# Weight splits, the order of the last pair, and out-projection weights through DRAM in the first layer of a streaming Conformer kernel

## Chip, cores and metric

The kernel runs on one core of a Trainium2 chip. The metric is the device time of one execution in microseconds (us). TensorE (PE), VectorE (DVE), ScalarE (ACT), GpSimd (POOL) and the queue of SyncE (SP), which issues nearly all DMAs, each work through their own list of instructions in order and wait for one another by semaphores.

## Reference

A two-layer encoder on 4096 prompt rows and 64 sample rows of width 1024. Only its first layer is touched by the change:

```
h = rmsnorm(x, pre_g)
z = h @ w_in + b_in                      # 1024 -> 3 x 1024
a, gl, gate = jnp.split(z, 3, axis=-1)
u = a * jax.nn.sigmoid(gl)
u_hist = jnp.concatenate([hist, u], axis=1)
c = depthwise_conv(u_hist, w_dw) + b_dw  # causal, 31 taps per channel
c = silu(layernorm(c, ln_g, ln_b)) * silu(gate)
y = c @ w_out + b_out
x = x + rmsnorm(y, post_g)
```

The second layer is sliding-window attention on the result, with its own projections.

## The kernel before

Every fp32 matrix is held as two fp16 parts, a high half and a low half, and each product is three fp16 matmuls (`mm3`): high by high, high by low, low by high. A weight's high half is a scaled copy by ACT or POOL (L161, L159), and its low half is one operation of DVE (L162) that reads the staged fp32 weight and the high half.

**Projections.** The prompt is cut into 8 blocks of 512 rows, taken two at a time: pair 0 is blocks 0 and 1, and so on to pair 3. For each block `in_jobs` loads four tiles of 128 rows (`x`), takes their norm, scales them (ACT, L483) and transposes them on PE (L207) into `hT`. A slot is one projection of 128 output channels for one block: 24 matmuls with 512 columns. Per channel group j (8 of them) there are three: `gl` (the gate of the gated unit; ACT takes the sigmoid, `sig`), `a` (the value; DVE multiplies it with `sig` into `u`, L774) and `gt` (the output gate; ACT takes the silu, `sg`, and a DMA puts it into `g_scr`). Three PSUM buffers carry the projections (`ps_mm`). `order(p)` writes the order of slots by hand: 48 in a pair. In pair 3 the eight `gt` slots of the second block are taken out into `tail`, after everything else.

**Convolution.** When both blocks of a pair have their `u` for group j, `conv_jobs` queues 31 taps over 1024 columns. Eleven go through ACT (products, L605) and POOL (adds into `pacc`, L614). Then ACT seeds the PSUM accumulator `acc` (L623, one buffer), and DVE adds 19 taps (L630), adds `pacc` (`join`, L641) and a DMA stores the result in `c_scr`. There are four buffers for `u`. `pump` doles out queued taps slot by slot, so the convolution of a pair runs on into the next pair.

**Other work at given slots.** `wjobs` gives the slot in pair 0 at which a quarter of a weight is loaded and split (`load_wa`: two loads of 512 KB into staging tiles `wst`, then eight high and eight low halves). `sched` gives the slots at which the rows of the next pair are loaded, normed, scaled and transposed. `big` (6 buffers) and `quad` (8 buffers) are pools of 4 KB per partition that staging tiles, `x`, `hT` and others share.

**Tail and layer norm.** After pair 3's slots, each of the eight `tail` slots is followed by one `w_oa_job` (load and split a piece of the out-projection weight, in the space where `w_a` was). `la_iter` runs the layer norm and out-projection of each 128 rows as a pipeline of steps (sums on POOL, statistics on PE into `lnb`, L264 to L317 on DVE, silu and the high half `hl` on ACT, L302 and L312, then products `psy`). Its first iterations stand in the last pair (`LA_LAST`) and the tail (`LA_TAIL`).

Within these rules a scheduler places the instructions of each engine at compile time, so neighbours on one engine may come from different slots.

## Time and profile before

| | us |
|---|---|
| median of three runs (2910.94, 2910.99, 2918.94) | 2910.99 |
| profiled execution | 2917.75 |
| its span, from first to last instruction | 2915.3 |
| PE busy in the span | 2765.5 |
| DVE busy in the span | 2251.6 |
| POOL busy in the span | 1680.8 |

In the span, pair 0 begins with the first projections at about 13.5 us, pair 3 ends and the tail begins at about 1075, the first `psy` product begins at 1124.1, and the second layer fills the stretch from about 1500 to the end. Rows of a profile give a start, a duration, the engine, the line, and the tiles written and read; "x8" is a count of instructions, and an arrow in brackets names what the engine waited for.

### The profile page before, as it was taken

The page shows a single profiled execution, that of the slowest core. Times are in us where ns is not written, and L with a number is a line of the kernel's source. Part 1 is how long each engine was busy: PE and PEld are TensorE (multiplying, and loading weights), DVE is VectorE, ACT ScalarE, POOL GpSimd, SP SyncE. Part 2 cuts the span into 40 slices and gives each one's busy share as a digit, 9 for nine tenths or more (in the row PEclk, how much of TensorE's full clock was granted, in tenths as well). Part 3 has the DMA queues.
Part 4 walks back from the last instruction along what each step waited for, and adds up shares of the span by engine and source line. Part 5 has one row for each costly group of instructions (what it writes and reads, how often), then busy time and mean ns, then how long its engine had stood idle before and what let it go on. Part 6 is the DMA issues. An engine that isn't in the chain of part 4 may idle for free.

```text
span 2915.3 us, 62257 instructions
## 1 busy us (share of the span) xinstructions
PE 2765.5 (95%) x24441; PEld 1793.6 (62%) x24441; DVE 2251.6 (77%) x3828; ACT 1785.7 (61%) x3957; POOL 1680.8 (58%) x1614
## 2 busy tenths in 40 slices
PE   7988999999999998999988999999999999999998
PEld 5433455444444443444447998998777777777775
DVE  5899888989988889979975777754676666666665
ACT  5666667666666566457764777654555555555554
POOL 4888578779877798977742344323334333333332
PEclk9999999999999999999999999999999999999999
DMA  5122111121120124666645666667323323433321
GB/s 169 53 80 69 53 54 49 39 68 48 46 80 29 44 67 139 207 189 188 207 155 174 211 207 222 209 198 233 99 94 113 115 99 99 128 104 96 114 72 60
DMA packets 256010, 341.16 MB, mean 117 GB/s; under 512 B 40069, under 2 KB 184197, under 8 KB 254949
## 3 DMA queue, kind: packets, MB, share of 16 engines
q1 hardware_dynamic: 255717, 337.20, 36.0%
q8 instruction: 191, 3.13, 0.4%
q14 instruction: 102, 0.84, 0.1%
HBM read 206.46 MB, written 130.72 MB: 116 GB/s over the span
## 4 chain that ended last, share of the span: by engine, by line
PE 32%; DVE 8%; ACT 5%; DMA 4%; POOL 2%; issue 2%; SPq 1%; POOLq 0%; ACTq 0%; DVEq 0%
PE sx_g L991 5%; PE psy L182 3%; PE psy L183 3%; PE psy L185 3%; PE sz_g L991 3%; PE ptr L1610 2%; PE pv L1644 2%; PE sx_q L991 2%; ACT p L1575 2%; PE sz_q L991 2%; PE sw_g L991 1%; PE sc L1544 1%; PE sc L1545 1%; DVE tTb L1112 1%; DVE x L1097 1%
## 5 line engine op out<-in xcount | busy, mean ns | idle before, releaser
L630 DVE SCALAR_TENSOR_TENSOR acc<-u,pt,acc 128x1024 f32<-128x1024 f32 x608 | 782.1, 1286 | 60.9 <-ACT acc L623 47.0
L614 POOL TENSOR_TENSOR pacc<-pacc,prods 128x1024 f32<-128x1024 f32 x213 | 505.9, 2376 | 105.6 <-ACT prods L605 95.3
L605 ACT ACTIVATE prods<-u,pt 128x1024 f32<-128x1024 f32 x213 | 241.9, 1144 | 94.6 <-POOL pacc L614 94.0
L1575 ACT ACTIVATE p<-p,st 128x192 f32<-128x192 f32 (+1 forms) x520 | 228.1, 441 | 80.6 <-DVE st L1569 80.2
L614 POOL TENSOR_TENSOR pacc<-pacc,pr 128x1024 f32<-128x1024 f32 x107 | 253.9, 2373 | 39.0 <-ACT pr L605 34.0
L182 PE MATMUL psy<-w_oa,hl 128*128 128x512 f16 x512 | 198.7, 388 | 20.4 <-ACT hl L312 14.9
L1548 DVE CUSTOM_DVE_ANT_0 p<-sc,bias 128x192 f32<-128x192 f32 (+1 forms) x520 | 159.7, 349 | 73.8 <-PE sc L1545 56.6
L1594 POOL TENSOR_TENSOR p<-p,st 128x768 f32<-128x768 f32 (+2 forms) x130 | 190.1, 1483 | 34.4 <-DVE st L1590 33.2
L190 PE MATMUL ps_gt<-hT,w_gt 128*128 128x512 f16 x512 | 197.0, 385 | 10.1 <-ACT w_gt L161 5.3
L192 PE MATMUL ps_a<-hT,w_a 128*128 128x512 f16 (+1 forms) x528 | 198.1, 375 | 3.2 <-DVE w_a L162 3.2
L183 PE MATMUL psy<-w_oa,hl 128*128 128x512 f16 x512 | 198.4, 388 | 2.1 <-DVE w_oa L162 2.1
L190 PE MATMUL ps_a<-hT,w_a 128*128 128x512 f16 (+1 forms) x528 | 198.1, 375 | 2.1 <-ACT sig L793 1.7
L190 PE MATMUL ps_gl<-hT,w_gl 128*128 128x512 f16 (+1 forms) x528 | 198.5, 376 | 1.7 <-ACT sig L793 1.1
L191 PE MATMUL ps_gl<-hT,w_gl 128*128 128x512 f16 (+1 forms) x528 | 197.9, 375 | 0.9 <-DVE hT L209 0.9
L192 PE MATMUL ps_gt<-hT,w_gt 128*128 128x512 f16 x512 | 195.8, 383 | 2.8 <-DVE w_gt L162 2.8
L191 PE MATMUL ps_a<-hT,w_a 128*128 128x512 f16 (+1 forms) x528 | 198.1, 375 | 0.0
L192 PE MATMUL ps_gl<-hT,w_gl 128*128 128x512 f16 (+1 forms) x528 | 197.9, 375 | 0.0
L182 PE MATMUL psy<-w_ob,ogT 128*128 128x512 f16 x512 | 195.1, 381 | 2.4 <-ACT ogT L1660 2.4
L191 PE MATMUL ps_gt<-hT,w_gt 128*128 128x512 f16 x512 | 196.9, 385 | 0.0
L183 PE MATMUL psy<-w_ob,ogT 128*128 128x512 f16 x512 | 195.1, 381 | 0.0
L991 PEld LDWEIGHTS <-w_qS 128*128 128x128 f16 x3072 | 180.2, 100 | 12.0 <-issue 11.7
L991 PEld LDWEIGHTS <-w_gS 128*128 128x128 f16 x3072 | 180.7, 98 | 6.0 <-issue 4.8
(363 smaller groups left out, 7120.6 us busy)
## 6 DMA issues: line engine op xcount, KB each, us to landing
x<-in_x_prompt SPq DMA_DIRECT2D x32, 512.0 KB, 3.4
g_scr<-sg SPq DMA_DIRECT2D x64, 256.0 KB, 2.0
c_scr<-c SPq DMA_DIRECT2D x32, 512.0 KB, 2.6
c<-c_scr SPq DMA_DIRECT2D x32, 512.0 KB, 4.5
g<-g_scr SPq DMA_DIRECT2D x32, 512.0 KB, 4.2
x<-x_scr SPq DMA_DIRECT2D x128, 128.0 KB, 3.6
h_scr<-hTb SPq DMA_DIRECT2D x32, 512.0 KB, 3.5
h_scr<-tTb SPq DMA_DIRECT2D x32, 512.0 KB, 4.7
```

Source lines behind the costliest of these rows:

```text
L182: nc.tensor.matmul(out, wts[i][0], mov[i][0], start=i == 0, stop=False)
L183: nc.tensor.matmul(out, wts[i][0], mov[i][1], start=False, stop=False)
L190: nc.tensor.matmul(out, wh, mh, start=i == 0, stop=False)
L191: nc.tensor.matmul(out, wh, ml, start=False, stop=False)
L192: nc.tensor.matmul(out, wl, mh, start=False, stop=i == n - 1)
L605: nc.scalar.activation(dst[:, :T], u[:, k : k + T], AF.Identity, scale=wdw[:, j, k : k + 1], bias=pt[:, j, R_DWB : R_DWB + 1] if k == 0 el ...
L614: nc.gpsimd.tensor_tensor(out=pacc[:, :T], in0=pacc[:, :T], in1=dst[:, :T], op=ALU.add)
L630: nc.vector.scalar_tensor_tensor(out=acc[:, :T], in0=u[:, k : k + T], scalar=wdw[:, j, k : k + 1], in1=acc[:, :T], op0=ALU.mult, op1=ALU.add,)
L991: nc.tensor.matmul(ps[:, j, :], w[:, wz, kb, j * P : j * P + P], rhs(rz, kb), start=first and j + kb + wz + rz == 0, stop=last and j == KH ...
L1548: nc.vector.tensor_tensor_reduce(out=pbuf[:, t, par * 192 + lo : par * 192 + 192], in0=ps[:, tt, :nk], in1=bias[:, lo:], scale=1.0, scalar ...
L1575: nc.scalar.activation(pp, pp, AF.Exp, scale=2.0 ** -(kv * 4 + t) / SQ, bias=st[:, 1, par, t : t + 1], accum_out=st[:, 3, par, t : t + 1],)
L1594: nc.gpsimd.tensor_tensor(out=pp, in0=pp, in1=st[:, 4, par, :, None].to_broadcast([P, 4, 3 * CH - lo]), op=ALU.mult)
```

## The change

1. The weights of `w_in` are split sooner: the ten quarters of `w_in` are loaded at slots 0, 2, 3, 5, 9, 12, 14, 16, 24 and 27 in place of 1, 7, 7, 8, 13, 19, 19, 20, 31 and 32. Those before slot 17 are staged in `quad` tiles, not `big` ones.
2. The convolution of groups 0 and 1 in pair 0 is done in two halves of 512 columns (`HALVES`), the first of them as soon as the first block's `u` is there.
3. In every pair but the last, groups 6 and 7 of the first block come before those of the second. In the last pair all `gl` and `a` come first, then the eight `gt` of the first block, then those of the second as before.
4. Loads, norms, scales and transposes of the next pair's rows get other slots; for the second block the scale is taken apart from the transposes by two slots.
5. The out-projection weight is split in pairs 1 and 2 instead of in the tail: `put_w_oa` loads a piece of 256 KB into a `big` tile, splits it into another (16 pieces, eight in each pair) and stores both halves in a DRAM scratch. In pair 3, at slot 32, four DMAs of 1 MB fetch them. The state output of the sample (`state_out`) moves from the end of pair 1 to slot 3 of pair 2.

```
+HALVES = 2
-LA_LAST = {36: -6, 39: -5, 43: -4}
+LA_LAST = {33: -6, 36: -5, 39: -4}
-OA_TAIL = (1, 1, 1, 1, 1, 1, 1, 1)
...
-        for g in range(4):
-            wjobs.setdefault(6 * g + 1, []).append(lambda g=g: load_wa(w_gt, 2 * D, 256 * g, 256))
-            if g < 3:
-                wjobs.setdefault(12 * g + 7, []).append(lambda g=g: load_wa(w_gl, D, 256 * (g + 1), 256))
-                wjobs.setdefault(12 * g + 8, []).append(lambda g=g: load_wa(w_a, 0, 256 * (g + 1), 256))
+        for m, dst, base, g in (
+            (0, w_gt, 2, 0), (2, w_gl, 1, 1), (3, w_a, 0, 1), (5, w_gt, 2, 1), (9, w_gt, 2, 2),
+            (12, w_gl, 1, 2), (14, w_a, 0, 2), (16, w_gt, 2, 3), (24, w_gl, 1, 3), (27, w_a, 0, 3),
+        ):
+            args = (dst, base * D, 256 * g, 256, quad if m < 17 else None)
+            wjobs.setdefault(m, []).append(lambda args=args: load_wa(*args))
 
         def order(p):
             out = []
+            if p == SB // 2 - 1:
+                out = [(k, h, j) for j in range(KB) for h in range(2) for k in ("gl", "a")]
+                return out + [("gt", h, j) for h in range(2) for j in range(KB)]
...
+            out += [(k, 0, j) for j in range(KB - 2, KB) for k in ("gl", "a")] + [("gt", 1, j) for j in range(4, 6)]
+            out += [(k, 1, j) for j in range(KB - 2, KB) for k in ("gl", "a")] + [("gt", 1, j) for j in range(6, 8)]
             return out
...
-                conv_jobs(b // 2, j, u, TC)
+                if b == 1 and j < HALVES:
+                    conv_jobs(0, j, u, TA, TA, True)
+                else:
+                    conv_jobs(b // 2, j, u, 0, TC, True)
+            elif b == 0 and j < HALVES:
+                conv_jobs(0, j, u, 0, TA, False)
...
+        def put_w_oa(g, k):
+            box = {}
+
+            def load():
+                t = box["t"] = big([P, D], F32, f"woa_{g}_{k}")
+                nc.sync.dma_start(out=t[:, :HN], in_=woa_v[:, k, g * HN : g * HN + HN])
+                box["w"] = big([P, 2, HN], F16, f"woas_{g}_{k}")
+
+            def comp():
+                st, w = box["t"][:, :HN], box["w"]
+                nc.scalar.activation(w[:, 0], st, AF.Copy, scale=SW)
+                nc.vector.scalar_tensor_tensor(
+                    out=w[:, 1], in0=st, scalar=SW, in1=w[:, 0], op0=ALU.mult, op1=ALU.subtract
+                )
+                nc.sync.dma_start(out=woa_scr[k // KH * 2 + g, :, :, k % KH, :], in_=w)
...
-                    for z, fn in zip((10, 13, 15, 16, 16), (a_[1][i], a_[2][i]) + a_[3][i]):
-                        sched.setdefault(z + 6 * i, []).append(fn)
...
+                    for z, fn in zip((14, 16, 19, 20, 20), (a_[1][i], a_[2][i]) + a_[3][i]):
+                        sched.setdefault(z + 5 * i, []).append(fn)
...
+            if p in (1, 2):
+                for z in range(8):
+                    load, comp = put_w_oa(p - 1, z)
+                    sched.setdefault(2 + 3 * z // 2, []).append(load)
+                    sched.setdefault(3 + 3 * z // 2, []).append(comp)
...
+                if p + 1 == NP and m == 2 * 2 * KB:
+                    w_oa = Weight("w_oa")
+                    for k in range(2):
+                        for g in range(2):
+                            nc.sync.dma_start(out=w_oa.t[k][g], in_=woa_scr[2 * k + g])
```

The lists of instructions show what this moves. The first place is DVE near its first convolution tap in pair 0. Names are tile, block or pair, group and a running number, so `u_0_0` is the first `u`, `acc_0_0` its accumulator, `w_gt_01` a piece of the `gt` weight; L162 before is L163 after, L630 is L631, L774 is L781. Before, from the last low halves ahead of the taps:

```order
L162 SCALAR_TENSOR_TENSOR w_a_10_81<-wst_817,gsc_73,w_a_10_81 128x256 x4
L774 SCALAR_TENSOR_TENSOR u_0_0_531<-ps_a_1_0_736,ba_109,sig_1_0_694 128x512
L162 SCALAR_TENSOR_TENSOR w_gt_01_88<-wst_1017,gsc_73,w_gt_01_88 128x256 x2
L630 SCALAR_TENSOR_TENSOR acc_0_0_798<-u_0_0_531,pt_102,acc_0_0_798 128x1024
L162 SCALAR_TENSOR_TENSOR w_gt_01_88<-wst_1017,gsc_73,w_gt_01_88 128x256 x2
L630 SCALAR_TENSOR_TENSOR acc_0_0_798<-u_0_0_531,pt_102,acc_0_0_798 128x1024 x2
```

The same place after:

```order
L781 SCALAR_TENSOR_TENSOR u_0_0_532<-ps_a_0_0_483,ba_110,sig_0_0_481 128x512
L163 SCALAR_TENSOR_TENSOR w_a_10_82<-wst_638,gsc_73,w_a_10_82 128x256 x2
L163 SCALAR_TENSOR_TENSOR w_a_00_80<-wst_628,gsc_73,w_a_00_80 128x256
L210 TENSOR_TENSOR hT_1_3_334<-pst_a1_0_1_342,hT_1_1_332 128x4x128
L163 SCALAR_TENSOR_TENSOR w_gt_00_88<-wst_747,gsc_73,w_gt_00_88 128x256
L163 SCALAR_TENSOR_TENSOR w_a_10_82<-wst_638,gsc_73,w_a_10_82 128x256
L163 SCALAR_TENSOR_TENSOR w_gt_00_88<-wst_747,gsc_73,w_gt_00_88 128x256
L163 SCALAR_TENSOR_TENSOR w_a_10_82<-wst_638,gsc_73,w_a_10_82 128x256
L163 SCALAR_TENSOR_TENSOR w_gt_00_88<-wst_747,gsc_73,w_gt_00_88 128x256
L631 SCALAR_TENSOR_TENSOR acc_0_0_553<-u_0_0_532,pt_103,acc_0_0_553 128x512
```

The first tap now follows the first block's `u` (`ps_a_0_0`), not the second's (`ps_a_1_0`); 19 low halves of 256 columns stand ahead of that first `u`, where there were none, and in all 64 of the 80 stand ahead of the first block of 1024-column taps.

The second place is DVE where the convolution of group 5 of pair 3 ends and that of group 6 runs beside the first layer-norm steps (L264, L298 and L310 before; one more after). Before:

```order
L641 TENSOR_TENSOR c_3_5_8721<-acc_3_5_8512,pacc_3_5_8464 128x1024
L630 SCALAR_TENSOR_TENSOR acc_3_6_8724<-u_6_6_8541,pt_102,acc_3_6_8724 128x1024 x2
L162 SCALAR_TENSOR_TENSOR w_oa_10_8814<-wst_8927,w_oa_10_8814 128x512 x2
L630 SCALAR_TENSOR_TENSOR acc_3_6_8724<-u_6_6_8541,pt_102,acc_3_6_8724 128x1024 x2
L282 TENSOR_SCALAR lnr_1_8971<-lnb_8624 128x1
L264 TENSOR_TENSOR c_2_8699<-c_2_8699,lnb_8624 128x1024
L298 TENSOR_TENSOR c_0_8501<-c_0_8501,lnb_8624 128x1024
```

After:

```order
L642 TENSOR_TENSOR c_3_5_8799<-acc_3_5_8637,pacc_3_5_8474 128x1024
L631 SCALAR_TENSOR_TENSOR acc_3_6_8837<-u_6_6_8471,pt_103,acc_3_6_8837 128x1024 x2
L283 TENSOR_SCALAR lnr_1_9179<-lnb_8913 128x1
L265 TENSOR_TENSOR c_2_9027<-c_2_9027,lnb_8913 128x1024
L631 SCALAR_TENSOR_TENSOR acc_3_6_8837<-u_6_6_8471,pt_103,acc_3_6_8837 128x1024
L299 TENSOR_TENSOR c_0_8788<-c_0_8788,lnb_8913 128x1024
```

The sixteen low halves of `w_oa` are gone from here, and the steps of the layer norm stand where they stood, relative to the convolution.

The third place is SP in pair 2, where pieces of the out-projection weight are loaded (L816, new) and stored (L825, new). Before, nothing of the kind stands on SP; after:

```order
L825 DMA woa_scr_79<-woas_1_0_5454 256x1x512
L816 DMA woa_1_1_5512<-in_a_w_out 128x512
L825 DMA woa_scr_79<-woas_1_1_5514 256x1x512
L816 DMA woa_1_2_5586<-in_a_w_out 128x512
L825 DMA woa_scr_79<-woas_1_2_5588 256x1x512
L816 DMA woa_1_3_5641<-in_a_w_out 128x512
L825 DMA woa_scr_79<-woas_1_3_5643 256x1x512
L816 DMA woa_1_4_5729<-in_a_w_out 128x512
L706 DMA g_scr_76<-sg_4_2_5726 128x512
L643 DMA c_scr_75<-c_1_7_5553 128x1024
```

Each load stands behind the store of the piece before it: with `hT_4` in four of the six `big` buffers, two are left for a piece and its halves. The stores of a gate (`sg_4_2`) and of a convolution result (`c_1_7`) stand behind four such loads.

More of the change, by code (lines that the diff above doesn't have):

```diff
@@ L119, in tile_streaming_conformer @@
     x1_scr = dpool.tile([NT, D], F32, name="x1_scr")
+    woa_scr = dpool.tile([4, P, 2, KH, HN], F16, name="woa_scr")
     def slot(shape, dt, name):
@@ L543, in tile_streaming_conformer, with load_wa @@
         a_w = ins["a_w_in"][0]
-        def load_wa(dst, base, c0, cn):
+        def load_wa(dst, base, c0, cn, room=None):
             step = 1024 // cn
             for k0 in range(0, KB, step):
-                st = big([P, step, cn], F32, "wst")
+                st = (room or big)([P, step, cn], F32, "wst")
                 split_weight(dst, a_w, st, list(range(k0, k0 + step)), base + c0, cn, c0, 0, True)
@@ L584, in tile_streaming_conformer, with conv_jobs @@
         LAG = 2
-        def conv_jobs(b, j, u, T):
-            t0 = bl[2 * b][0]
+        def conv_jobs(b, j, u, o, T, last):
+            t0 = bl[2 * b][0] + o
             cd = (T + 124) / 960.0
@@ L606, in run @@
                         dst[:, :T],
-                        u[:, k : k + T],
+                        u[:, o + k : o + k + T],
                         AF.Identity,
@@ L623, in seed @@
                 nc.scalar.activation(
-                    box["acc"][:, :T], u[:, k : k + T], AF.Identity, scale=wdw[:, j, k : k + 1], bias=0.0
+                    box["acc"][:, :T], u[:, o + k : o + k + T], AF.Identity, scale=wdw[:, j, k : k + 1], bias=0.0
                 )
@@ L630, in run @@
                     nc.vector.scalar_tensor_tensor(
-                        out=acc[:, :T], in0=u[:, k : k + T], scalar=wdw[:, j, k : k + 1], in1=acc[:, :T],
+                        out=acc[:, :T], in0=u[:, o + k : o + k + T], scalar=wdw[:, j, k : k + 1], in1=acc[:, :T],
                         op0=ALU.mult, op1=ALU.add,
@@ L638, in join @@
                 clock["pacc"] -= 1
-                clock["u"] -= 1
+                clock["u"] -= last
                 out = pa.tile([P, TC], F32, tag="cout", name=f"c_{b}_{j}", bufs=1)
@@ L745, in order @@
                 out += [(k, 1, j) for j in range(2) for k in ("gl", "a")] + [("gt", 0, j) for j in range(2, 4)]
-            for j in range(0 if p else 2, KB):
+            for j in range(0 if p else 2, KB - 2):
                 A, B = [("gl", 0, j), ("a", 0, j)], [("gl", 1, j), ("a", 1, j)]
@@ L795, in sig_slot @@
             )
+        woa_v = ins["a_w_out"][0].rearrange("(k p) n -> p k n", p=P)
+        def put_w_oa(g, k):
[11 more added lines that the diff above has]
+                nc.sync.dma_start(out=woa_scr[k // KH * 2 + g, :, :, k % KH, :], in_=w)
+            return load, comp
         sigs, ubox = {}, {}
@@ L803, in tile_streaming_conformer @@
             if late_prep:
-                for z, fn in zip((0, 0, 0, 1, 1, 1), late_prep):
+                for z, fn in zip((0, 0, 1, 1), late_prep):
                     sched.setdefault(z, []).append(fn)
@@ L810, in tile_streaming_conformer @@
                 for i in range(4):
-                    for z, fn in zip((10, 13, 15, 16, 16), (a_[1][i], a_[2][i]) + a_[3][i]):
-                        sched.setdefault(z + 6 * i, []).append(fn)
-                for z, i in ((39, 0), (41, 1)):
+                    for z, fn in zip((14, 16, 19, 20, 20), (a_[1][i], a_[2][i]) + a_[3][i]):
+                        sched.setdefault(z + 5 * i, []).append(fn)
+                for i, z in enumerate((34, 36, 43, 45)):
                     sched.setdefault(z, []).append(b_[1][i])
-                for i in range(2):
-                    for fn in (b_[2][i],) + b_[3][i]:
-                        sched.setdefault(44 + i, []).append(fn)
-                    sched.setdefault(45 + i, []).append(b_[1][2 + i])
-                for fn in (b_[2][2],) + b_[3][2]:
-                    sched.setdefault(47, []).append(fn)
-                late_prep = [b_[2][3], *b_[3][3]]
+                for i, z in enumerate((36, 37, 45, 46)):
+                    sched.setdefault(z, []).append(b_[2][i])
+                for i, z in enumerate((40, 41, 46, 47)):
+                    for fn in b_[3][i][:1]:
+                        sched.setdefault(z, []).append(fn)
+                for i, z in enumerate((42, 43)):
+                    for fn in b_[3][i][1:]:
+                        sched.setdefault(z, []).append(fn)
+                late_prep = [*b_[3][2][1:], *b_[3][3][1:]]
             if p == 0:
                 hTs, l, nm, tr = in_jobs(SB)
-                for z, fn in zip((36, 37, 38, 38, 38), (l[0], nm[0]) + tr[0]):
+                for z, fn in zip((30, 31, 33, 33, 33), (l[0], nm[0]) + tr[0]):
                     sched.setdefault(z, []).append(fn)
@@ L863, in tile_streaming_conformer @@
             sjobs.popleft()()
-        w_oa = Weight("w_oa")
-        oaj = deque((c0, k0) for c0 in (0, 512) for k0 in range(0, KB, 2))
-        def w_oa_job():
-            c0, k0 = oaj.popleft()
-            st = big([P, 2, 512], F32, "wst")
-            split_weight(w_oa, ins["a_w_out"][0], st, [k0, k0 + 1], c0, 512, c0, None)
         ec = [slot([P, 2, D], F32, f"early_{z}") for z in range(4)]
@@ L878, in tile_streaming_conformer @@
                 la_iter(ti, la_fns)
-            for _ in range(OA_TAIL[q_] if q_ < len(OA_TAIL) else 0):
-                if oaj:
-                    w_oa_job()
             gate_slot(*args)
@@ L885, in tile_streaming_conformer @@
             pump(dq, "d", TAIL_D)
-        while oaj:
-            w_oa_job()
         for ti in range(EARLY):
```

3 lines of the change are left out of this document (2 added, 1 removed).

## The prediction

> **What bounds the kernel now.** I read the totals first, then the busy time by stage, then what PE waited for in the stages where it loses time, then DVE in those stages.
>
> ```profile
> span 2915.3 us, 62257 instructions
> PE 2765.5 (95%) x24441; PEld 1793.6 (62%) x24441; DVE 2251.6 (77%) x3828; ACT 1785.7 (61%) x3957; POOL 1680.8 (58%) x1614
> ```
>
> PE is busy for 95% of the span, so the change can only take from PE's idle time and from its slow clock, and only in the stages that it touches. The windows show them (columns: stretch, its us, then busy us and count of PE, PEld, DVE, ACT, POOL, then PE's granted clock, DMA share, GB/s):
>
> ```profile
> 0.00:63.00 63.00, 47.66 (x272) 31.24 (x273) 35.48 (x84) 37.97 (x76) 32.52 (x60) 0.92 0.51 165
> 63.00:136.00 73.00, 73.00 (x391) 38.27 (x390) 60.25 (x58) 49.16 (x60) 60.72 (x33) 1.00 0.22 73
> 136.00:349.00 213.00, 186.66 (x936) 87.25 (x934) 200.22 (x184) 139.03 (x177) 164.10 (x97) 0.96 0.21 70
> 349.00:843.00 494.00, 491.74 (x2743) 236.91 (x2742) 439.18 (x424) 320.37 (x389) 394.42 (x235) 1.00 0.14 49
> 843.00:890.00 47.00, 40.17 (x187) 19.80 (x186) 41.46 (x37) 31.66 (x40) 36.37 (x28) 0.93 0.33 101
> 890.00:1075.00 185.00, 185.00 (x860) 84.07 (x859) 162.32 (x137) 110.87 (x119) 152.06 (x70) 1.00 0.13 43
> 1075.00:1118.00 43.00, 41.11 (x199) 19.36 (x197) 38.69 (x35) 30.40 (x42) 41.96 (x26) 1.00 0.31 98
> 1118.00:1255.00 137.00, 119.40 (x547) 56.00 (x547) 125.58 (x120) 74.45 (x135) 117.84 (x111) 0.94 0.62 194
> ```
>
> In each I take idle time (stretch less PE busy) plus the part of the stretch that the clock is short of 1.00. For 136 to 349, the body of pair 0 and the start of pair 1: 213 − 186.66 = 26.3, and 0.04 × 213 = 8.5, together **34.9**. For 843 to 890, the boundary of pairs 2 and 3: 6.8 + 3.3 = **10.1**. For 1075 to 1255, the tail and the first layer-norm products: 1.9 + 17.6 + 8.2 = **27.7**. Between them PE is full. The first 63 us lose 15 and some clock to loads and first transposes. So 72.7 us are within reach; the second layer and the rest of the first keep their instructions, and I leave them as they are. The clock is low only in the stretches with idle time, and I let it follow that time.
>
> Then what PE waited for, first from 63 to 349, then from 843 to 1255 (total us, times, longest):
>
> ```profile
> PE pst_a L207 <- ACT x L483: 8.5, 2, 4.6
> PE ps_gt L190 <- ACT w_gt L161: 5.3, 2, 3.6
> PE ps_gt L190 <- DVE u L774: 4.0, 1, 4.0
> PE ps_a L192 <- DVE w_a L162: 3.2, 4, 1.0
> PE ps_gt L192 <- DVE w_gt L162: 2.8, 2, 1.7
> PE ps_a L190 <- ACT sig L793: 1.7, 1, 1.7
> ```
>
> ```profile
> PE psy L182 <- ACT hl L312: 12.1, 6, 4.0
> PE pst_a L207 <- ACT x L483: 6.6, 2, 4.1
> PE psy L183 <- DVE w_oa L162: 2.1, 1, 2.1
> ```
>
> In pair 0 the weight halves cost 11.3, the two steps behind a late `u` or `sig` 5.7, and transposes whose rows were scaled too late 8.5. At the boundary it is transposes again. In the tail it is `hl`, the end of the layer norm's chain, which passes DVE many times; DVE is 92% busy from 1118 to 1255 (125.58 of 137) and 94% from 136 to 349. So beside the transposes **DVE is what PE waits for**, and the question is how much work leaves DVE there.
>
> **The change part by part.** *Pair 0: weights split sooner, convolution in halves.* One row for a low half alone, one for a piece beside POOL's adds, and the windows of L162 alone (busy of DVE, count, then clock, DMA share, GB/s):
>
> ```profile
> 40.00:80.00 40.00, 15.45 (x34) 1.00 0.38 119
> 80.00:260.00 180.00, 55.52 (x46) 0.97 0.21 72
> ```
>
> ```profile
> 173.53 1.27 DVE L630 SCALAR_TENSOR_TENSOR acc<-u,pt,acc 128x1024 f32<-128x1024 f32 x1
> 174.72 7.53 DVE L162 SCALAR_TENSOR_TENSOR w_a<-wst,gsc,w_a 128x256 f16<-128x256 f32 x3
> L614 POOL TENSOR_TENSOR pacc<-pacc,prods 128x1024 f32<-128x1024 f32 x213 | 505.9, 2376 | 105.6 <-ACT prods L605 95.3
> L162 DVE SCALAR_TENSOR_TENSOR w_a<-wst,gsc,w_a x16: 469/692/2575, 171.8 to 249.9; 128x256 f16<-128x256 f32 x16
> ```
>
> Ahead of the convolution a low half takes 15.45 / 34 = 0.454 us. Beside it, 55.52 / 46 = 1.207, and three of them 7.53: a low half reads two SBUF tiles, and waits out an add of 2.376. Taps, with `acc` in PSUM, stay at 1.286. All 80 cost 71.0 now. After the change 19 stand ahead of the first `u`, 45 between it and the last of the two halved groups, and 16 in the full convolution. The 45 are not free of adds: the halves bring the adds forward as well, at half the width. With m for their mean, the 80 cost 19 × 0.454 + 45m + 16 × 1.207 = 27.9 + 45m.
>
> ```profile
> 80.25 1.29 DVE L630 SCALAR_TENSOR_TENSOR acc<-u,pt,acc 128x1024 f32<-128x1024 f32 x1 [3.09 <-ACT acc L623]
> 40.00:80.00 40.00, 40.00 (x248) 24.43 (x246) 21.60 (x44) 20.98 (x35) 16.46 (x16) 1.00 0.38 119
> L630 DVE SCALAR_TENSOR_TENSOR acc<-u,pt,acc 128x1024 f32<-128x1024 f32 x608 | 782.1, 1286 | 60.9 <-ACT acc L623 47.0
> L774 DVE SCALAR_TENSOR_TENSOR u<-ps_a,ba,sig 128x512 f32<-128x512 f32 x64 | 47.7, 746 | 14.2 <-PE ps_a L192 14.2
> ```
>
> The halves cost DVE something. No tap of 512 columns is in the trace; by the row of `u`, also 512 columns with one operand in PSUM, I take 0.746. For two groups, 38 times (2 × 0.746 − 1.286) = 7.8; two seeds more at 47.0 / 28 = 1.7 (the waits for a seed at L623, all but four of the 32) = 3.4; and two joins more at some 0.2 each beyond their columns: 11.6. They also give DVE something: taps now start after the first block's `u` at 41, not at 80.25, and from 40 to 80 DVE is idle for 40 − 21.60 = 18.4. DVE's standing in pair 0 so changes by 27.9 + 45m − 71.0 + 11.6 − 18.4 = **45m − 49.9**. At m = 0.454 that is −29.5; at 2.575, with each waiting out a full add, +66. I take 0.692, the median of the row of `w_a` in pair 0, since adds at half width block for less: **−19**. At most −29 counts, since of the 34.9 the sample's transposes keep some 6 (its scale and transposes still stand in one slot: half of the 8.5, with its share of clock).
>
> *The start.* The 19 low halves ahead of the first `u` take 8.6, and the row stands next to idle time:
>
> ```profile
> 36.67 0.44 DVE L527 COPY pt<-pst_rows 128x268 f32<-128x268 f32 x1 [3.95 <-PE pst_rows L524]
> 40.33 0.75 DVE L774 SCALAR_TENSOR_TENSOR u<-ps_a,ba,sig 128x512 f32<-128x512 f32 x1 [1.91 <-PE ps_a L192]
> wst<-in_a_w_in SPq DMA_DIRECT2D x6, 512.0 KB, 8.1
> ```
>
> 5.9 of it fits in these two gaps; **+3** (bounds 0 and +8). The last row, of the DMA issues up to 40 us, has six loads, landing in 8.1; six more are issued by slot 5, behind the rows of both blocks on SP's queue.
>
> *The boundary.* Scales now stand two slots ahead of their transposes, 2 × 5.2 us by the 24 products of a slot at 0.216 (5.18). Both waits of 6.6 in total, and the clock with them, go: **−9** of 10.1. If ACT is later than two slots, nothing goes.
>
> *Out-projection pieces in pairs 1 and 2.* Sixteen low halves come to a stretch where DVE works 439.18 of 494:
>
> ```profile
> L162 DVE SCALAR_TENSOR_TENSOR w_oa<-wst,w_oa x16: 679/956/2581, 1086.8 to 1146.7; 128x512 f16<-128x512 f32 x16
> ```
>
> Each takes 0.68 alone and 2.58 beside adds, 10.9 to 41.3 in all. DVE's idle time there is 54.8, of which 16 seeds at 1.7 are not free: 27.6 are left. At 1.43 each (0.68, and the 0.75 that low halves of pair 0 gain beside adds) it is 22.9, hidden in those 27.6; I charge **+3** for pieces at bad places, bounds 0 and +14 (41.3 − 27.6). Without that cover it would be the 22.9. ACT's sixteen high halves lie in its idle time (320.37 of 494). On SP, loads wait for stores over two buffers, with gate and result stores queued behind; there are 12 slots, 62 us, for eight pieces, 7.8 each.
>
> The Trainium skill says in "SBUF — State Buffer", section "SBUF: two separate sides", that VectorE and GpSimd share one pair of ports as an exclusive lock: a VectorE operation with two SBUF inputs and a GpSimd operation that reads SBUF block each other for the whole instruction, whichever starts first. This case's trace agrees (7.53 for three). That speaks against moving this split into pairs 1 and 2, where adds are frequent: by the rule a low half among back-to-back adds waits half an add on average, 0.68 + 1.19 = 1.87, an estimate, so 29.9 for the sixteen, 7 more than the 22.9 above.
>
> *The tail.* DVE loses the sixteen low halves and their waits. In the windows they took:
>
> ```profile
> 1080.00:1150.00 70.00, 18.13 (x16) 0.93 0.47 152
> ```
>
> Also, the last `u` come eight slots earlier, 41 us, since the `gt` of the first block now follow them. DVE can use that as far as it is idle from 890 to 1075: 22.7, less six seeds at 1.7, 12. Together it enters the layer norm some 30 us ahead. But the chain of one iteration through sums, DVE and ACT to `hl` stays as long, and its first steps stand at the same places relative to the convolution; waits for `hl` of up to 4.0 may be that chain alone. I take a little over half of 27.7: **−15**, bounds −5 and −26.
>
> *Edits at nothing.* The four 1 MB fetches of `w_oa` are issued after slot 32 of pair 3, some 16 slots and the eight of the tail, 83 to 125 us, ahead of the first `psy`; the DMA share there is 0.13. At 3.8 us for 512 KB they need about 30. The moved state output and the order of groups 6 and 7 change no count; PE has its three PSUM buffers for the second.
>
> **Sum**, against the profiled execution of 2917.75: +3 − 19 − 9 + 3 − 15 = −37. That execution is 6.8 above the median 2910.99; I take the same difference from the median: **2874**, its own range 2858 to 2886.
>
> **The rivals.** *DVE stays the bound.* m is 0.82 (0.454 and a share of a half-width add), the out-projection pieces pay fully, the start too: +8 − 13 − 9 + 14 − 15 = −15, **2896**. For it: 200.22 of 213 busy. Against it: 11.3 of the waits name weights, which now come earlier whatever DVE does.
>
> *Nearly all waits go.* −29 − 10 − 26 = −65, **2846**. For it: lateness of DVE up to two slots (10.4) is taken up by three PSUM buffers, so a part of its saving counts in full. Against it: the `hl` chain.
>
> *The split is not in fact sooner.* Six more loads of 512 KB at 3.8 delay the rows behind them by up to 22.8, so the start pays 20 and pair 0 gains 14, the tail 7: 20 − 14 − 9 + 3 − 7 = −7, **2904**, within 0.3% of no change, about what a measurement can tell. For it: the DMA share of 0.51 up to 63. Against it: it is short of full, and DVE is idle beside it.
>
> *Slower.* The 45 low halves meet adds after all, since the halved groups start POOL's adds near 45 us, where the first now comes at 77.22:
>
> ```profile
> 77.22 2.36 POOL L614 TENSOR_TENSOR pacc<-pacc,prods 128x1024 f32<-128x1024 f32 x1 [0.57 <-ACT prods L605]
> ```
>
> With the out-projection pieces at their upper end too, the sum is 45m − 49.9 + 3 − 9 + 14 − 15 = 45m − 57: it turns at m = 1.27, and at 1.55 gives +13, **2924**. For it: 1.207 beside adds today, three at 2.5 in a row. The Trainium skill's rule on the shared ports, named above, is this mechanism; the trace has it for full adds only. Against it: an add of 512 columns blocks for about half as long, and the adds fill only a part of 41 to 80.
>
> **How the numbers follow.** Forecast .45, DVE stays the bound .20, nearly all gone .17, not sooner .10, slower .08. Faster by over 0.3% (below 2902) are the first three, .82; same .10; slower .08. The range goes from 2842, a little below the second rival with all terms at their best ends, to 2904, with the third at its edge; the slower case and the odd miss are left out.
>
> **What would show it.** The first tap near 50, not 80. L162 (then L163) in 40 to 100: m at 0.7 or at 1.3. No PE waits for `w_gt` or `w_a`, and for `x` only the sample's; from 136 to 349 PE idle near 12, not 26. In pairs 1 and 2 the sixteen low halves near 1.4, with no new waits of PE. In the tail no `w_oa`, waits for `hl` about half, and the first `psy` about 22 sooner than now:
>
> ```profile
> 1124.07 0.39 PE L182 MATMUL psy<-w_oa,hl 128*128 128x512 f16 x1 [1.82 <-ACT hl L312]
> ```
>
> I am wrong if PE's idle time moves to the first 63 us, if pairs 1 and 2 lose more than 5, or if the second layer moves by more than 5.

## The result and the profile after

The changed kernel takes 2891.52 us (median of four runs, 2889.01 to 2893.14), the kernel before 2914.97 in four runs; the ratio is 0.9914, 95% interval 0.9898 to 0.9930. That is 23.5 us less; the forecast was 37 less, 2874 (its own range 2858 to 2886), in a range of 2842 to 2904 for all cases together. The profiled execution took 2892.36, 25.4 below the one before.

The totals, and the busy time by stage at the same clock times as before (us, PE, PEld, DVE, ACT, POOL, PE's granted clock, DMA share, GB/s). From the middle of pair 0 on, the changed kernel is further in its work at the same clock time:

```profile
span 2890.6 us, 62399 instructions
PE 2762.4 (96%) x24441; PEld 1795.7 (62%) x24441; DVE 2248.4 (78%) x3868; ACT 1783.4 (62%) x3973; POOL 1687.3 (58%) x1634
```

```profile
0.00:63.00 63.00, 46.99 (x260) 30.68 (x261) 48.59 (x110) 45.62 (x92) 48.73 (x73) 0.89 0.73 236
136.00:349.00 213.00, 203.67 (x1034) 96.43 (x1033) 191.41 (x177) 138.59 (x179) 149.17 (x84) 0.97 0.24 80
349.00:843.00 494.00, 483.00 (x2699) 233.64 (x2698) 440.24 (x427) 323.51 (x400) 385.14 (x235) 1.00 0.17 58
843.00:890.00 47.00, 44.70 (x207) 20.70 (x206) 42.02 (x38) 32.99 (x37) 45.49 (x27) 0.96 0.24 68
1118.00:1255.00 137.00, 122.76 (x583) 59.22 (x582) 123.65 (x115) 70.87 (x135) 120.98 (x124) 0.98 0.59 178
```

In pair 0 (136 to 349) PE's idle time fell from 26.3 to 9.3. In pairs 1 and 2 (349 to 843), where PE lost 2.3, it now loses 11.0. What PE waits for, first in pair 0, then from 349 to 843, then from the tail to the end of the out-projection (total us, times, longest):

```profile
PE ps_gt L191 <- DVE u L781: 2.5, 1, 2.5
PE ps_gl L191 <- DVE u L781: 2.1, 1, 2.1
PE ps_gl L191 <- ACT hT L209: 2.1, 1, 2.1
PE ps_gt L191 <- ACT sig L805: 1.9, 1, 1.9
PE pst_a L208 <- ACT x L484: 1.7, 1, 1.7
```

```profile
PE pst_a L208 <- DVE hT L210: 3.6, 1, 3.6
PE ps_gt L191 <- ACT sig L805: 3.2, 2, 1.9
PE ps_gl L191 <- DVE u L781: 1.7, 2, 1.5
PE ps_gt L191 <- DVE u L781: 1.7, 1, 1.7
```

```profile
PE lnb L281 <- POOL csq L275: 14.6, 12, 5.5
PE psy L183 <- ACT hl L313: 7.8, 5, 2.9
```

Of the 11.0, the wait of 3.6 lies behind 800 and belongs to the boundary of pairs 2 and 3, which now comes sooner; the waits for `u` and `sig` are a loss that the kernel before did not have. No weight is waited for any more. In the tail the waits for `hl` have about halved, from 14.9 to 7.8, and those for POOL's sums of squares (`csq`) have grown from 10.9 to 14.6:

```profile
PE psy L182 <- ACT hl L312: 14.9, 7, 4.0
PE lnb L280 <- POOL csq L274: 10.9, 13, 1.3
```

Windows at equal clock times mix the stages of two kernels once one is ahead. So I also compare when the same operation ends in both traces. The u are counted from 1 to 64, 16 to a pair. Two such rows, the last u of pair 0 and the last of pair 2, in the trace before:

```profile
309.26 0.75 DVE L774 SCALAR_TENSOR_TENSOR u<-ps_a,ba,sig 128x512 f32<-128x512 f32 x1
...
852.11 0.74 DVE L774 SCALAR_TENSOR_TENSOR u<-ps_a,ba,sig 128x512 f32<-128x512 f32 x1
```

and in the trace after:

```profile
290.38 0.74 DVE L781 SCALAR_TENSOR_TENSOR u<-ps_a,ba,sig 128x512 f32<-128x512 f32 x1
...
841.73 0.75 DVE L781 SCALAR_TENSOR_TENSOR u<-ps_a,ba,sig 128x512 f32<-128x512 f32 x1
```

The lead is 18.9 at the first and 10.4 at the second. All along the program (ends in us):

| operation | before | after | difference |
|---|---|---|---|
| 3rd u | 74.7 | 81.8 | +7.1 |
| 6th u (group 2 of pair 0) | 120.5 | 122.9 | +2.4 |
| 16th u, end of pair 0 | 310.0 | 291.1 | -18.9 |
| 20th u, in pair 1 | 394.0 | 381.2 | -12.8 |
| 34th u, in pair 2 | 640.1 | 624.2 | -15.9 |
| 36th u, in pair 2 | 668.4 | 660.0 | -8.4 |
| 48th u, end of pair 2 | 852.9 | 842.5 | -10.4 |
| first output gate of the tail | 1085.3 | 1070.6 | -14.7 |
| last output gate of the tail | 1133.6 | 1112.9 | -20.7 |
| last psy | 1532.6 | 1505.7 | -26.9 |
| span | 2915.3 | 2890.6 | -24.7 |

From the 6th u on pair 0 gains 21, the tail and the out-projection 12, the stretch from the end of pair 2 to the tail 4. Pairs 1 and 2 give back 8.5, in two steps: 6 by the 20th u, and 7.5 between the 34th and the 36th; between the steps 3 are gained.

### The profile page after: what moved, and what is told of

Its sections match the earlier page's. It is cut to its first block, busy times and chain, and to the rows that moved or that the text cites. A ratio compares the mean times of both kernels' runs of the same rounds, so it can differ in the third digit from the quotient of the medians.

```text
span 2890.6 us, 62399 instructions
## 1 busy us (share of the span) xinstructions
PE 2762.4 (96%) x24441; PEld 1795.7 (62%) x24441; DVE 2248.4 (78%) x3868; ACT 1783.4 (62%) x3973; POOL 1687.3 (58%) x1634
## 5 line engine op out<-in xcount | busy, mean ns | idle before, releaser
L631 DVE SCALAR_TENSOR_TENSOR acc<-u,pt,acc 128x1024 f32<-128x1024 f32 (+1 forms) x646 | 790.7, 1224 | 73.0 <-ACT acc L624 57.2
L615 POOL TENSOR_TENSOR pacc<-pacc,prods 128x1024 f32<-128x1024 f32 (+1 forms) x227 | 510.9, 2253 | 105.8 <-ACT prods L606 89.3
L606 ACT ACTIVATE prods<-u,pt 128x1024 f32<-128x1024 f32 (+1 forms) x227 | 246.1, 1093 | 102.7 <-POOL pacc L615 102.1
L615 POOL TENSOR_TENSOR pacc<-pacc,pr 128x1024 f32<-128x1024 f32 (+1 forms) x113 | 254.5, 2253 | 42.4 <-ACT pr L606 30.7
L1580 DVE CUSTOM_DVE_ANT_0 p<-sc,bias 128x192 f32<-128x192 f32 (+1 forms) x520 | 159.7, 350 | 92.9 <-PE sc L1577 74.7
L1023 PEld LDWEIGHTS <-w_qS 128*128 128x128 f16 x3072 | 179.7, 99 | 11.9 <-issue 11.5
```

The lines of the kernel that those rows point to most:

```text
L606: nc.scalar.activation(dst[:, :T], u[:, o + k : o + k + T], AF.Identity, scale=wdw[:, j, k : k + 1], bias=pt[:, j, R_DWB : R_DWB + 1] if k ...
L615: nc.gpsimd.tensor_tensor(out=pacc[:, :T], in0=pacc[:, :T], in1=dst[:, :T], op=ALU.add)
L631: nc.vector.scalar_tensor_tensor(out=acc[:, :T], in0=u[:, o + k : o + k + T], scalar=wdw[:, j, k : k + 1], in1=acc[:, :T], op0=ALU.mult, o ...
L1023: nc.tensor.matmul(ps[:, j, :], w[:, wz, kb, j * P : j * P + P], rhs(rz, kb), start=first and j + kb + wz + rz == 0, stop=last and j == KH ...
L1580: nc.vector.tensor_tensor_reduce(out=pbuf[:, t, par * 192 + lo : par * 192 + 192], in0=ps[:, tt, :nk], in1=bias[:, lo:], scale=1.0, scalar ...
```

## The experiments

Each kernel is read in two ways: by its time, beside runs of the kernel before on the same chip, and by its lead at the places above. The chips differ a little: the kernel before took 2914.97 to 2918.46 on them. So a difference between two medians holds to some 3 us, and the ratios allow for that. The second layer has the same code in all of them, yet from the last psy on the profiles differ by up to 9 us (1379.1 to 1387.8); a difference of a few us at the end of one profile is not read. All leads at one place, for reference (us against the kernel before, negative is ahead):

| kernel | time | end of pair 0 | 20th u | 36th u | end of pair 2 | last psy |
|---|---|---|---|---|---|---|
| changed kernel | 2891.52 | -18.9 | -12.8 | -8.4 | -10.4 | -26.9 |
| e_nohalves | 2904.37 | -9.4 | +1.8 | +8.3 | +6.4 | -11.0 |
| e_oldw | 2899.89 | -5.9 | +1.7 | +6.7 | +4.2 | -13.7 |
| e_oldw_nohalves | 2915.82 | +5.3 | +11.1 | +17.7 | +15.5 | -3.3 |
| e_oldprep | 2910.48 | -14.7 | -7.2 | -2.6 | -1.5 | -6.9 |
| e_before_prep | 2925.27 | +0.1 | -0.2 | -2.7 | -0.8 | +7.4 |
| e_woa_tail | 2892.32 | -18.8 | -22.6 | -22.6 | -24.0 | -22.7 |
| e_oldlast | 2902.86 | -20.1 | -14.4 | -9.9 | -12.3 | -12.7 |
| e_oldlast_woa_tail | 2896.82 | -17.6 | -21.4 | -22.0 | -23.5 | -21.7 |
| e_quad2 | 2881.64 | -18.1 | -12.5 | -11.1 | -14.1 | -33.6 |
| e_low_pool | 2884.91 | -18.3 | -18.6 | -15.8 | -18.8 | -36.5 |
| e_pool8 | 2886.38 | -18.8 | -13.2 | -11.9 | -14.9 | -32.8 |

### Pair 0: halves and weights

```
-HALVES = 2
+HALVES = 0
```

> Changed kernel with HALVES = 0: no group of pair 0 is convolved in halves. Theory A (by the terms of the prediction the halves use 18.4 us of DVE's idle time and cost 11.6): pair 0 ends 5 to 9 us later than in the changed kernel, 2896 to 2900. Rival B (the low halves fill DVE between 41 and 76 us now, so the taps of the halves only delay u, 7 us late at the third u, and low halves, and pay 11.6 for nothing): 3 to 10 us faster, 2882 to 2888, and the third u is back at 75 us.

Measured: 2904.37, ratio to the kernel before 0.9954 (0.9940 to 0.9968), 13 us slower than the changed kernel, more than Theory A expected; pair 0 ends 9.5 later, and PE waits for `u` again (11.2 in three waits, 63 to 360). Rival B falls: the third u is indeed back at 75.9, but what the halves cost there is small beside what they give. The windows from 40 to 100 us, of this kernel first, then of the changed one, show where the gain is:

```profile
40.00:100.00 60.00, 60.00 (x346) 34.08 (x344) 35.06 (x60) 33.72 (x55) 30.35 (x26) 1.00 0.39 129
```

```profile
40.00:100.00 60.00, 57.93 (x338) 33.31 (x336) 56.85 (x98) 43.28 (x75) 52.95 (x46) 1.00 0.40 131
```

Without halves DVE is idle for 25 of the 60 us; with them for 3. Those 22 us of work, less the 11.6 that the halves were reckoned to cost, are 10, an estimate that lies near the 9.5.

```
-            (0, w_gt, 2, 0), (2, w_gl, 1, 1), (3, w_a, 0, 1), (5, w_gt, 2, 1), (9, w_gt, 2, 2),
-            (12, w_gl, 1, 2), (14, w_a, 0, 2), (16, w_gt, 2, 3), (24, w_gl, 1, 3), (27, w_a, 0, 3),
+            (1, w_gt, 2, 0), (7, w_gl, 1, 1), (8, w_a, 0, 1), (7, w_gt, 2, 1), (13, w_gt, 2, 2),
+            (19, w_gl, 1, 2), (20, w_a, 0, 2), (19, w_gt, 2, 3), (31, w_gl, 1, 3), (32, w_a, 0, 3),
...
-            args = (dst, base * D, 256 * g, 256, quad if m < 17 else None)
+            args = (dst, base * D, 256 * g, 256)
```

> Changed kernel with the ten weight quarters loaded at the slots of the kernel before and staged where it stages them; halves stay. Theory A (the earlier split saves 71 - 58 = some 13 us of low halves on DVE and the 11.3 us in which PE waited for weights): pair 0 ends 12 to 22 us later than in the changed kernel, 2903 to 2913, and PE waits for w_gt and w_a again. Rival B (pair 0 is shorter by the halves alone): within 4 of 2891.

Measured: 2899.89, ratio 0.9938 (0.9926 to 0.9951). At the end of pair 0, 13.0 of the lead of 18.9 are gone, and 13.2 are still missing at the last psy, as Theory A has it; the time rises by 8 only. The difference lies behind the last psy, where this profile takes 1379.1 and that of the changed kernel 1384.9; why is not shown. PE waits for weights again, from 63 to 360:

```profile
PE ps_gl L193 <- DVE w_gl L163: 4.6, 1, 4.6
...
PE ps_a L193 <- DVE w_a L163: 2.1, 1, 2.1
```

Both undone together (the same two edits):

> Changed kernel with weights at the old slots and without halves. Singly, no halves cost 13 us and old weight slots 8. Theory A (the two add up, as the terms of the prediction do): 2910 to 2914, and pair 0 ends as late as in the kernel before. Rival B (each is of use only with the other, since halves fill DVE while weights are split and the earlier split clears DVE for the taps): 2902 to 2906, no later than without halves alone.

Measured: 2915.82, ratio 0.9991 (0.9980 to 1.0002). Pair 0 now ends 5.3 behind the kernel before, 24.2 behind the changed one; singly they lost 9.5 and 13.0. So the two **add up**, and the whole gain of pair 0 is theirs. The 5.3 are what the other edits cost by there; which one is not shown, but it is not the schedule of the next rows alone, since the old one makes the end of pair 0 later by 4.2 (e_oldprep).

### The schedule of the next rows

The list of slots for loads, norms, scales and transposes is put back:

```
-                    for z, fn in zip((14, 16, 19, 20, 20), (a_[1][i], a_[2][i]) + a_[3][i]):
-                        sched.setdefault(z + 5 * i, []).append(fn)
...
+                    for z, fn in zip((10, 13, 15, 16, 16), (a_[1][i], a_[2][i]) + a_[3][i]):
+                        sched.setdefault(z + 6 * i, []).append(fn)
```

> Changed kernel with the loads, norms, scales and transposes of the next pair's rows at the slots of the kernel before. Theory A (transposes right behind their scale make PE wait 4 us or so at each of the boundaries that showed it): waits of PE for scaled rows come back, 6 to 9 us at the boundary of pairs 2 and 3 and 4 at that of pairs 0 and 1, and the time rises by 5 to 12, to 2896 to 2903. Rival B (PE only waits there for what it would wait for behind, DVE's u): the waits come back, the time stays within 3 of 2891.

Measured: 2910.48, ratio 0.9975 (0.9965 to 0.9986): 19 us slower than the changed kernel, more than Theory A expected. From 63 to 900 PE waits six times for a scaled row:

```profile
PE pst_a L208 <- ACT x L484: 18.2, 6, 5.9
```

That is more than the 15.1 of four such waits in the kernel before: with weights, pieces and the new order beside it, the old schedule is worse than it was. The opposite, the new schedule in pairs 1 and 2 of the kernel before:

```
+                if p:
+                    for i in range(4):
+                        for z, fn in zip((14, 16, 19, 20, 20), (a_[1][i], a_[2][i]) + a_[3][i]):
...
+            if p == SAMP_AT // 2 + 1:
+                sched.setdefault(3, []).append(lambda: state_out(cv_s[0, 0], halo_s))
...
-                state_out(cv_s[0, 0], halo_s)
```

> Kernel before, with the new slots for loads, norms, scales and transposes of the next rows in pairs 1 and 2 only, and with the state output of the sample at slot 3 of pair 2. Theory A (the prediction's term: scale and transposes apart take 9 of the 10.1 us lost at the boundary of pairs 2 and 3): 5 to 10 us faster than the kernel before on the same chip. Rival B (the schedule is worth its 19 us only beside the other edits, which leave PE waiting for nothing else there): within 4 of the kernel before.

Measured: 2925.27, ratio 1.0020 (1.0008 to 1.0033), 7 us slower than before. Theory A falls, and the time is worse than the 4 that Rival B allowed. From 840 to 900 PE has no wait above the profile's floor, so the waits at the boundary do go; yet the lead at the first gate of the tail is 2.8, and by the last psy it is a loss of 7.4, with these rows between 290 and 1500:

```profile
PE psy L182 <- ACT hl L312: 13.2, 5, 4.5
...
PE psy L183 <- DVE w_oa L162: 7.0, 2, 5.3
PE lnb L292 <- POOL dg L285: 5.9, 4, 3.0
```

In the kernel before the waits for `hl` were 14.9, those for `w_oa` 2.1 and those for `dg` 2.0: the first have shrunk, the other two have grown by 8.8 together. So what the boundary gained the tail took. That this is for the low halves that DVE has there is argued, not shown: no run takes them alone out of this kernel.

### The out-projection weight and the order of the last pair

The weight goes back to the tail:

```
-            if p in (1, 2):
-                for z in range(8):
-                    load, comp = put_w_oa(p - 1, z)
...
+            if oaj:
+                w_oa_job()
             gate_slot(*args)
```

> Changed kernel, with the out-projection weight split in the tail as in the kernel before; the new order of the last pair stays. Theory A (the tail's gain of some 12 us, from the last output gate to the last product of the out-projection, comes from the low halves that left DVE there): the lead stays near -15 through pair 2, and the tail gives back 8 us or more, so the time is 2889 to 2895. Rival B (it comes from the new order, which gives the convolution its last inputs 41 us sooner): the lead through pair 2 stays too and the tail keeps 8 us or more of its gain, so the time is 2881 to 2887.

Measured: 2892.32, ratio 0.9917 (0.9900 to 0.9934), the time of the changed kernel. But nothing else is the same: the lead at the end of pair 2 is 24.0 in place of 10.4, and from there to the last psy it shrinks by 1.3 where the changed kernel gains 16.5. PE waits for `hl` from 1060 to 1520:

```profile
PE psy L183 <- ACT hl L313: 18.4, 8, 5.7
```

So **the pieces cost 13.6 in pairs 1 and 2**, and with the new order the low halves' leaving is worth 17.8 from there to the last psy. In the time nothing is left of it: moved as it is, the split gains nothing. With the old order the pieces cost much the same, 11.2 (e_oldlast against e_oldlast_woa_tail, below). Theory A, as far as the time goes; the lead was not expected to grow to 24.

```
-LA_LAST = {33: -6, 36: -5, 39: -4}
+LA_LAST = {36: -6, 39: -5, 43: -4}
...
-                out = [(k, h, j) for j in range(KB) for h in range(2) for k in ("gl", "a")]
-                return out + [("gt", h, j) for h in range(2) for j in range(KB)]
```

> Changed kernel with the slot order of the last pair and the places of its first layer-norm steps as in the kernel before; the out-projection weight is still split in pairs 1 and 2, and its four fetches stand behind the last pair, since w_a is in use until then. Theory A (the tail's gain comes from the low halves that left DVE): within 4 of 2891. Rival B (it comes from the new order): 8 to 13 us slower, 2899 to 2904, with waits for hl again.

Measured: 2902.86 (2890.25 to 2909.61 in eight runs), ratio 0.9947 (0.9932 to 0.9963). It gains 0.4 from the end of pair 2 to the last psy. That looks like rival B, but e_woa_tail has the new order and gains nothing either. Two reservations: the profile is of the execution that took 2909.61, 6.8 above the median, so its leads may be too small by that much; and here the state output after the last pair makes PE wait once for 6.9, and the fetches stand later.

> Both parts undone: old order of the last pair and the out-projection weight split in the tail. Both theories: the lead at the end of pair 2 stays near -15 and the tail adds nothing to it, 2893 to 2900. If the two parts add up, its time is that of the two single runs less that of the changed kernel; if one covers the other, it is above that.

Measured: 2896.82, ratio 0.9932 (0.9913 to 0.9951), between e_woa_tail and e_oldlast, with an interval that overlaps both. From the end of pair 2 it loses 1.8. The four runs for that stretch: both parts +16.5, new order alone -1.3, low halves gone alone +0.4, neither -1.8. **While the low halves are in the tail, the new order gives it nothing**; with them gone it gives 16.1, or 9 if e_oldlast's profile is 6.8 too late. What the low halves' leaving gives in the old order, 2.2 or up to 9 by the same reckoning, is not settled, nor is why the order needs it. Neither theory had this. The times cannot settle it: the sum of the single times (2892.32 + 2902.86 - 2891.52 = 2903.66) is 6.8 above the measured 2896.82, but the sum of the ratios, 0.9950, still lies inside the interval of the measured one.

### What the pieces cost in pairs 1 and 2

The step in pair 2 stands where ACT, whose list is in order, waits for loads of pieces. Waits of ACT from 585 to 680 in the changed kernel, and its timeline over one piece:

```profile
ACT woas L821 <- DMA woa<-in_a_w_out: 16.2, 6, 6.5
```

```profile
654.61 2.01 DVE L822 SCALAR_TENSOR_TENSOR woas<-woa,woas 128x512 f16<-128x512 f32 x1 [0.42 <-ACT woas L821]
...
656.64 0.53 SPq L825 DMA_DIRECT2D woa_scr<-woas  x1
657.26 0.56 SPq L816 DMA_DIRECT2D woa<-in_a_w_out  x1
...
661.04 0.63 ACT L821 ACTIVATE woas<-woa 128x512 f16<-128x512 f32 x1 [6.47 <-DMA woa<-in_a_w_out]
661.58 0.20 ACT L793 COPY halo_p<-u 128x30 f32<-128x30 f32 x1
661.69 1.24 ACT L606 ACTIVATE pacc<-u,pt 128x1024 f32<-128x1024 f32 x1
```

The store waits for the low half, the next load is issued behind the store, and ACT stands for 6.47 at the next high half, with the copy of `u` and the first product of the next group queued behind it.

```
-                t = box["t"] = big([P, D], F32, f"woa_{g}_{k}")
+                room = quad if g else big
+                t = box["t"] = room([P, D], F32, f"woa_{g}_{k}")
...
-                box["w"] = big([P, 2, HN], F16, f"woas_{g}_{k}")
+                box["w"] = room([P, 2, HN], F16, f"woas_{g}_{k}")
```

> Changed kernel, but in pair 2 the pieces of the out-projection weight and their halves are staged in the pool of 8 buffers, where 4 are free, in place of the 2 left in the pool of 6. Theory A (a ring on two buffers: load waits store, store waits low half, low half stands behind taps, and ACT's in-order list stands at the piece whose load is late): ACT's waits for loads of pieces in pair 2 fall from 16.2 us to under 5, the lead over the kernel before at the u of groups 2 and 3 of pair 2 stays near -14 instead of shrinking to -5 to -8, and the time falls by 4 to 8, to 2884 to 2888. Rival B (the low halves' own time on DVE, 11.6 us in pair 2, is what makes u late): ACT's waits fall too, but the lead shrinks as before and the time stays within 2 of 2891.

Measured: 2881.64 (2881.15 to 2884.60), ratio 0.9878 (0.9864 to 0.9891), below the changed kernel's interval. ACT's waits for the loads:

```profile
ACT woas L822 <- DMA woa<-in_a_w_out: 4.2, 3, 1.7
```

Theory A in the main: 12.0 of the waits are gone, PE's own waits from 590 to 680 fall from 3.9 to 0.3, and the lead shrinks by 2.3 between the 34th u (-13.4) and the 36th, not by 7.5. Some of it is lost sooner, though: from the 32nd u, the end of pair 1, to the 36th the lead falls by 3.8 here (from 14.9) and by 6.8 in the changed kernel (from 15.2). The eight low halves also take 9.72 in place of 11.59, so a part may be theirs, as Rival B has it. By leads it is worth 3.7 at the end of pair 2 and 6.7 at the last psy; the rest of its 10 us lies in the second layer, within what differs there anyway. **This kernel beats both others.**

That leaves the 6 us lost by the 20th u, where pair 1's pieces have four more buffers.

```
+                    nc.gpsimd.tensor_scalar(st, st, scalar1=SW, scalar2=None, op0=ALU.mult)
+                    nc.gpsimd.tensor_tensor(out=w[:, 1], in0=st, in1=w[:, 0], op=ALU.subtract)
```

> The kernel with pair 2's pieces in the pool of 8 (2881.64), and in pair 1 the low halves of the pieces made by POOL, in two operations (scale in place, subtract), instead of one by DVE. With the split left in the tail, the lead at the fourth u of pair 1 is 22.6 us, with the pieces 12.9. Theory A (those 9.7 are the 13.4 us of DVE time of the eight low halves, at a place where DVE is what PE waits for): the lead there grows from 12.5 to 18 or more, and the time falls by 4 to 8, to 2874 to 2878. Rival B (they come from the high halves in ACT's list or the waits on SP's queue, or POOL's added work blocks DVE as much): the lead stays within 3 of 12.5 and the time at 2880 or above.

Measured: 2884.91 (2880.18 to 2887.23), ratio 0.9883 (0.9862 to 0.9904), no gain over e_quad2. The lead tells the mechanism: 18.6 at the 20th u, as Theory A has it. From 290 to 400, this kernel first, then the changed one, in which the eight low halves are DVE's:

```profile
290.00:400.00 110.00, 107.77 (x749) 53.95 (x747) 87.24 (x81) 75.89 (x99) 103.25 (x60) 0.98 0.26 85
```

```profile
290.00:400.00 110.00, 103.51 (x705) 51.73 (x704) 102.23 (x91) 73.08 (x96) 83.95 (x41) 0.97 0.25 80
```

DVE drops by 15.0, PE gains 4.3 of busy time. In the changed kernel PE is idle there for 6.5, and its clock is 0.03 short of 1.00 for 110 us, which by estimate is 3.3 more: together the 9.8 between its lead and that of e_woa_tail, whose PE is busy for 109.86 there at a clock of 1.00. So of those 9.8 some 6 are shown to hang on the place of the low halves on DVE; the rest is open. But of the 6 us at that place 3 are left by the last psy, and none can be told in the time. ACT's waits for the loads of pieces from 290 to 560, 5.5 in e_quad2, are now

```profile
ACT woas L822 <- DMA woa<-in_a_w_out: 14.2, 4, 5.8
```

The remedy isn't one: the two operations on POOL probably keep the buffers longer, which no run takes apart.

### POOL in the tail

```
+            n = POOL_TAPS - 3 if b == 3 and j >= 6 else POOL_TAPS
```

> The kernel with pair 2's pieces in the pool of 8 (2881.64), and in groups 6 and 7 of the last pair three taps moved from POOL to DVE. Theory A (behind the change PE waits in the tail and after it for the sums of squares on POOL, 14.9 us, because POOL's adds of the last groups stand ahead of them): six adds of 2.4 leave POOL, PE's waits for csq fall to 10 or less, and the time falls by 3 to 6, to 2876 to 2879. Rival B (DVE, which is 90% busy there, is as late as POOL): six taps of 1.29 on DVE make hl later, waits for hl grow by what those for csq lose, and the time is within 2 of 2882 or above.

Measured: 2886.38 (2883.08 to 2887.39), ratio 0.9895 (0.9879 to 0.9910), no faster than e_quad2 and by the medians 5 slower, with intervals that overlap. From 840 to 1500 PE waits for

```profile
PE psy L183 <- ACT hl L313: 10.8, 5, 3.5
PE lnb L281 <- POOL csq L275: 7.7, 10, 2.1
```

In e_quad2 it was 7.8 for `hl` and 14.9 for `csq`. Rival B as far as the time goes: of the 7.2 that `csq` loses, `hl` takes 3.0. The last psy still ends 0.8 later than in e_quad2. PE's clock from 1100 to 1500 was 0.97 in place of 0.98, by estimate 4 us, which would take the rest back. Taps moved from POOL to DVE give nothing here.

## Why the prediction was right

The time fell, and lies in the stated range. But 2891.52 is 5.5 above the forecast's own range, and the rival "DVE stays the bound", 2896, came nearer than 2874. And one of the three signs of being wrong came true: pairs 1 and 2 lose more than 5, by leads 8.5. The other two did not: PE's idle time up to 63 us is 16.0 where it was 15.3, and the second layer moved by 2.2.

- **The bound** was read rightly: PE full but for three stretches, DVE the engine behind it. That showed in pair 0 and at the start of pair 1 (e_nohalves, e_low_pool); in pair 2 it was in part ACT's list (e_quad2), and in the tail POOL came beside DVE.
- **Pair 0**, forecast -19: -21.3 from the 6th to the 16th u. The formula, 45m - 49.9, was right in its parts. The half-width tap took 0.754, where 0.746 was taken from the row of `u`. The 45 low halves between the first u and the full taps:

```profile
44.00:92.00 48.00, 22.50 (x45) 1.00 0.39 129
```

  m is 0.50, not 0.692, and not for the reason given, that adds at half width block for less: nearly all of the 45 ran before the second of the adds (last section). By the formula m of 0.50 is -27.4, with the start's +2.4 -25.0; the two parts together are worth 24.2 by e_oldw_nohalves. The other edits, put at nothing, cost 5.3 in pair 0. That -16 for start and pair 0 came so near the -18.9 is luck: an m taken too high made up for a cost left out.
- **The start**, +3: +7 at the third u, +2.4 at the sixth.
- **The boundary**, -9: the lead grows from 9.1 at the last output gate of pair 2 (863.0 before, 853.9 after) to 14.7 at the tail's first, -5.6. The waits for scaled rows went, as forecast. But the term was taken for a thing by itself. Alone it gives nothing (e_before_prep), and beside the other edits its absence costs 19, by the ratios 18 (e_oldprep).
- **The out-projection pieces**, +3, bounds 0 and +14: this is **the term that was mis-sized**. They cost 13.6 by e_woa_tail, nearly the upper bound. The low halves' own size was about right, 1.56 each where 1.43 was taken:

```profile
300.00:560.00 260.00, 13.39 (x8) 0.99 0.19 66
570.00:700.00 130.00, 11.59 (x8) 1.00 0.23 73
```

  The cover was wrong. The 27.6 of idle time on DVE was a sum over pairs 1 and 2; DVE's idle time lies in good part at the end of pair 1, 13.3 us in 40, and the pieces stand at the start of each pair, where only 2.3 and 2.6 in 40 are free. In the kernel without pieces (e_woa_tail):

```profile
300.00:340.00 40.00, 39.86 (x277) 20.48 (x276) 37.69 (x39) 26.16 (x34) 31.66 (x18) 1.00 0.20 63
...
540.00:580.00 40.00, 40.00 (x193) 18.94 (x192) 26.67 (x38) 24.73 (x30) 29.28 (x32) 1.00 0.17 61
580.00:620.00 40.00, 40.00 (x199) 19.57 (x198) 37.37 (x40) 27.76 (x33) 38.26 (x25) 1.00 0.21 70
```

  And the two buffers, named with 7.8 us of spacing a piece, were checked for SP's queue, not for ACT, which stood in order at the late loads. The prediction's estimate by the rule of the Trainium skill's page "SBUF — State Buffer", section "SBUF: two separate sides", half an add of waiting and so 1.87 a piece, was above the 1.56 measured, and would have made the sixteen only 7 us dearer, 2.3 of it beyond the 27.6 that were to cover them: what was wrong is mainly the place, not the duration.
- **The tail**, -15: -12.2 from its first gate to the last psy. The waits for `hl` halved as written, and `csq` on POOL took part of their place, which was not foreseen. That the new order gives the tail nothing while the low halves are there was not foreseen either; the prediction took them together. The first psy came 17 sooner, not 22.
- **The sum**: with the pieces at +14 in place of +3, the terms give -26, near the -25.4 of the profiled executions. But that the other terms fit so well is in part luck. By the leads it is -18.9 to the end of pair 0 (forecast -16), +8.5 in pairs 1 and 2 (+3), -4.3 from there to the tail's first gate (-9), -12.2 to the last psy (-15) and +2.2 behind it (0): -24.7, with misses both ways. The rival "DVE stays the bound" priced the pieces at +14 and pair 0 too low.

## What to carry to other kernels

Idle time of an engine covers added work only where it lies: sum it stage by stage, at the slots where the new work will stand. When a piece of work goes through several engines on few buffers, look at every in-order list in which a step of it waits, not only at the DMA queue. Two edits that touch the same bound should be tried together and apart; here one pair added up, and in another the new order was worth nothing until the low halves had left. And before a mean is explained by what else the window holds, look at the rows in order of time: two groups in one window need not have met.
